# Conditioning weights of one decoder layer loaded and summed for pairs of chunks

## The chip, the cores and the metric

The kernel runs on one core of a Trainium2 chip. The metric is the device time of one execution in microseconds. The median of three runs of the kernel before is 515.8 us (514.55 to 515.91).

## What is computed

One layer of a decoder over 256 tokens of width 1024, all in fp32. What matters here is its first step:

```
mod = silu(c) @ w_ada + b_ada            # w_ada: 1024 x 6144; six parts of 1024: shift1, scale1, gate1, shift2, scale2, gate2
u   = rmsnorm(x, norm1) * (1 + scale1) + shift1
proj = u @ w_in                          # w_in: 1024 x 6848; retention q|k|v|gate, MLA c_q|c_kv|k_rope, two branch gates
...                                      # retention, latent attention, output projections, residual
u2  = rmsnorm(h, norm2) * (1 + scale2) + shift2
h  += gate2 * hier_moe(u2)               # 4 groups of 8 experts, top 1 group, top 2 experts
out = rmsnorm(h, final_norm)
```

The change concerns only shift1 and scale1, the first two parts of mod (columns 0 to 2047 of w_ada).

## The kernel before

SBUF tiles come from 27 slots of 128 partitions by 2048 fp32 (1 MB each), PSUM tiles from 8 banks of 512 columns. All large loads go through one list, `LD`, and are issued by SyncE in the order in which they were added, as soon as a slot is free by a plan made in a first pass over the program. A slot is reused when its last reader is through, so an operation that writes a tile may have to wait for another engine.

The width of 1024 is worked off in eight chunks of 128. For chunk k the early part needs three loads: `("ada", k)`, 128 columns of shift1 and 128 of scale1 of all 1024 rows of w_ada (rows of 512 B, `ld_ada_early`); `("e0", k)`, 704 columns of w_in for c_q, c_kv and k_rope; and `("e1", k)`, 512 columns of w_in for retention's q. They are added in the order ada 0, x, ada 1, e0 0, e1 0, ada 2, e0 1, e1 1, and so on.

`ada_mm(k)` multiplies silu(c) with the loaded columns: eight matmuls of 256 columns, each on one of four groups of 32 columns of the array, so that four partial sums land at partitions 0, 32, 64, 96; DVE copies the bank to `ev`. `mod_of(k)` transposes `ev` (two transposes), and DVE adds the partial sums and makes the chunk's scale `acl` and shift `shc` (a reduction and two small operations). `x_turned(k)` transposes the normed x of the chunk. `u_of(k)` makes u of the chunk on ACT, rounds it to fp32r (`hi`), and DVE subtracts to get the rest (`lo`).

Every product is done as three fp32r matmuls (hi x hi, lo x hi, hi x lo). So each piece of w_in is split first: `split` rounds on ACT and subtracts on DVE (L469, L470). The loop over k (from L541) then does for each chunk: the splits of e0's two halves (352 columns each) and of e1 (512 columns); if there is a next chunk, `x_turned(k + 1)` and `ada_mm(k + 1)`; the products with the first half, `mod_of(k + 1)` and `u_of(k + 1)`, the products with the second half, 12 matmuls of 352 columns in all (L384 to L386); and twelve matmuls of 256 columns with e1 (L536 to L538).

In this stretch TensorE's order is the order of the code. ACT's and DVE's order is chosen by the framework's scheduler, and each of these engines works through its own queue in order. Behind the loop come the units of the middle part (the remaining products of u, attention, retention), then the routing, and the experts, whose weights stream in to the end.

Of the kernel before, what the change touches and what calls it, by code (L numbers as in the profile page):

```python
# [13 lines left out]
AF = mybir.ActivationFunctionType  # L14
ALU = mybir.AluOpType
AX = mybir.AxisListType
# [192 lines left out]
def body(ctx, tc, A, out, plan=None):  # L209
    nc = tc.nc  # L210
    T, V, S, G, Q = nc.tensor, nc.vector, nc.scalar, nc.gpsimd, nc.sync
# [5 lines left out]
    LD = Loads(SL, plan)  # L217
    ring = Ring(SL)

    def bank(name="bank"):  # L220
        return PB.alloc(name)

    w_ada = A["w_ada"][0].rearrange("(k p) n -> p k n", p=128)
# [4 lines left out]
    ev_s = SL.alloc("ev")  # L228
    csb = ev_s.t[:, 1024:1280].rearrange("p (k m) -> p k m", k=8)
# [4 lines left out]
    def row_load(r0, name, n0=0, n=None):  # L234
        v = A[name].rearrange("o n -> (o n)") if len(A[name].shape) == 2 else A[name]
        n = n or v.shape[0]
        S.dma_start(rows[r0:r0 + n // 128, :], v[n0:n0 + n].rearrange("(r c) -> r c", c=128))
# [3 lines left out]
    def ld_ada_early(k):  # L241
        def fn(t):
            v = t.rearrange("p (k s n) -> p k s n", k=8, s=2)
            for s in range(2):
                Q.dma_start(v[:, :, s, :], w_ada[:, :, s * 1024 + k * 128:s * 1024 + (k + 1) * 128])  # L245
        return fn
# [19 lines left out]
    row_load(16, "b_ada", 0, 2048)  # L266
    row_load(32, "q_norm")
    row_load(35, "kv_norm")
    for k in range(8):
        if k < 7:  # L270
            LD.add(("ada", k + 1), ld_ada_early(k + 1))
        LD.add(("e0", k), ld_k(w_in[:, k:k + 1, 4096:4800]))
        LD.add(("e1", k), ld_k(w_in[:, k:k + 1, 0:512]))
    uq = A["w_uq"][0].rearrange("(k p) n -> p k n", p=128)
# [8 lines left out]
    i = 0  # L283
# [78 lines left out]
    def small(n):  # L362
        if sml_n[0] + n > 256:
            sml_n[0] = 0
        a = sml[:, sml_n[0]:sml_n[0] + n]
        sml_n[0] += n
        return a
# [57 lines left out]
    def ada_mm(k, pa):  # L425

        ev = ev_s.t[:, 256 * (k % 2):256 * (k % 2 + 1)]
        t = LD.get(("ada", k)).t.rearrange("p (k n) -> p k n", k=8)
        for j in range(8):
            i = T.matmul(pa.t[32 * (j % 4):32 * (j % 4) + 32, :256], csb[:, j, :], t[:, j, :], start=j < 4, stop=j >= 4,  # L430
                         skip_group_check=True, tile_position=(0, 32 * (j % 4)))
        LD.done(("ada", k))
        V.tensor_copy(ev, pa.t[:, :256])
        return ev, i.ins

    def x_turned(k):
        px = bank()
        for b in range(2):
            T.transpose(px.t[:, b * 128:(b + 1) * 128], xh[:, b, k * 128:(k + 1) * 128], ident)
        return px  # L440

    last_u = [None]
# [1 line left out]
    def mod_of(k, pa, ev):  # L444
        for i in range(2):
            T.transpose(pa.t[:, 256 + i * 128:256 + (i + 1) * 128], ev[:, i * 128:(i + 1) * 128], ident)
        sc = small(2)
        V.tensor_reduce(sc, pa.t[:, 256:512].rearrange("p (i j r) -> p i j r", i=2, j=4)[:, :, :, 0], AX.X, ALU.add)
        V.scalar_tensor_tensor(acl[:, k:k + 1], sc[:, 1:2], bsc1[:, k:k + 1], colt[:, 8 + k:9 + k], op0=ALU.add,
                               op1=ALU.mult)  # L450
        V.tensor_add(shc[:, k:k + 1], sc[:, 0:1], colt[:, 16 + k:17 + k])
        pa.free()

    def u_of(k, px):
        last_u[0] = S.activation(uf[:, k, :], px.t[:, 0:256], AF.Identity, bias=shc[:, k:k + 1], scale=acl[:, k:k + 1]).ins
        hi, lo = hi_lo("u", k)
        S.activation(hi, uf[:, k, :], AF.Copy)
        V.tensor_tensor(lo, uf[:, k, :], hi, ALU.subtract)
        px.free()

    u_blk = blk_of("u")

# [62 lines left out]
    pa = bank()  # L525
# [16 lines left out]
    for k in range(8):  # L542
        hl = hl0 if k == 0 else []
        for w in early_w(k)[len(hl):]:
            hl.append(split(w, 352))
        LD.done(("e0", k))
        hl.append(split(LD.get(("e1", k)).t[:, :512].rearrange("p (k n) -> p k n", k=1), 512))
        LD.done(("e1", k))

        if 0 < k < 7:  # L550
            px, pa = x_turned(k + 1), bank()
            ev = ada_mm(k + 1, pa)[0]
        for n in range(2):
            s, hi, lo = hl[n]
            for b in range(2):
                mm3(eacc[n][b].t[:, :352], u_blk(k, b), (hi[:, 0, :], lo[:, 0, :]), k == 0, k == 7)
            s.free()
            if (n, k) == (0, 0):
                start.close()
                early = ExitStack()  # L560
                early.enter_context(tc.manual_schedule(engines={T.engine}))
                px = x_turned(1)
            if n == (k == 0) and k < 7:
                mod_of(k + 1, pa, ev)
                u_of(k + 1, px)
        if k == 0:
            eacc.append([bank("acc") for _ in range(2)])
        s, hi, lo = hl[2]
        feat_mm(eacc[2], hi[:, 0, :], lo[:, 0, :], *hi_lo("u", k), k)
        s.free()  # L570
    early.close()
    LD.margin = MARGIN[1]
    u_s.free()
# [1185 lines left out]
```

## Time and profile before

| | before |
|---|---|
| median of three runs | 515.8 us |
| profiled execution | 515.37 us, of which the span is 513.7 us |
| TensorE (PE) busy | 486.0 us, 95% of the span |
| VectorE (DVE) busy | 284.0 us, 55% |
| ScalarE (ACT) busy | 199.9 us, 39% |
| bytes moved by DMA | 174.86 MB, 340 GB/s in the mean |
| granted TensorE clock, mean | 0.989 |

The span runs from the first to the last instruction of the profiled execution; what lies around it is 1.67 us. PEld is TensorE's loading of weights, which overlaps its matmuls. A name such as `s<-in_w_ada` says that a tile of the slots was written from the input w_ada.

### The profile page before, as it was taken

To read this page: it belongs to the slowest core of one execution; us is meant where nothing else is said; L and a number is where in the kernel's file an instruction comes from. 1 tells how busy PE (TensorE), PEld (TensorE's weight loads), DVE (VectorE), ACT (ScalarE), POOL (GpSimd) and SP (SyncE) were. 2 spreads that over 40 slices of the span, in tenths; PEclk is the share of its full clock that TensorE was granted. 3 is DMA by queue.
4 is the path that set the end of the run, shared out by engine and by line. 5 is a ranking of instruction groups with operands and counts; after the bars stand their busy time and mean duration, and the time that the engine had idled before them with its cause. 6 is when DMAs were issued, how large, how long until landed. Compare 5 with 4: busy or idle time off the path is not lost.

```text
span 513.7 us, 8596 instructions
## 1 busy us (share of the span) xinstructions
PE 486.0 (95%) x3432; PEld 340.0 (66%) x3432; DVE 284.0 (55%) x529; ACT 199.9 (39%) x371; POOL 61.7 (12%) x59
## 2 busy tenths in 40 slices
PE   6999999999999999999999999999999799979874
PEld 2778999997787888888888887453544445334332
DVE  2555689894696997984777746434333131312013
ACT  2545773553678454456534423122112020112013
POOL 1000322411000002105872000000000000000000
PEclk8999999999999999999999999999999899999998
DMA  9999999888967592899698888999999999999993
GB/s 270 325 318 358 321 327 399 320 291 311 358 226 289 187 385 85 303 385 374 234 365 329 315 356 319 404 417 420 416 420 421 414 417 417 422 419 418 394 342 126
DMA packets 68098, 174.86 MB, mean 340 GB/s; under 512 B 5422, under 2 KB 27091, under 8 KB 57816
## 3 DMA queue, kind: packets, MB, share of 16 engines
q1 hardware_dynamic: 65602, 174.01, 90.6%
q10 hardware_dynamic: 2454, 0.27, 0.4%
q8 instruction: 28, 0.46, 0.4%
q14 instruction: 14, 0.11, 0.1%
HBM read 173.22 MB, written 1.05 MB: 339 GB/s over the span
## 4 chain that ended last, share of the span: by engine, by line
PE 60%; DMA 23%; SPq 6%; DVE 5%; ACT 1%; issue 1%; POOL 1%; ACTq 1%; DVEq 0%; POOLq 0%
DMA s<-in_w 21%; PE b L384 10%; PE b L386 10%; PE b L385 10%; PE b L1442 4%; SPq L253 4%; PE b L1554 3%; PE b L1382 2%; SPq L245 2%; PE b L1565 2%; DMA s<-in_w_in 1%; PE b L538 1%; PE b L537 1%; PE b L536 1%; DVE s L470 1%
## 5 line engine op out<-in xcount | busy, mean ns | idle before, releaser
L470 DVE TENSOR_TENSOR s<-s,s 128x1024 fp32r<-128x1024 f32 (+2 forms) x92 | 103.4, 1136 | 42.9 <-ACT s L469 42.7
L469 ACT ACTIVATE s<-s 128x1024 fp32r<-128x1024 f32 (+2 forms) x92 | 83.5, 923 | 80.1 <-PE b L386 51.0
L384 PE MATMUL b<-s,s 128*128 128x512 f32 (+2 forms) x258 | 101.8, 395 | 1.1 <-ACT s L469 1.0
L386 PE MATMUL b<-s,s 128*128 128x512 f32 (+2 forms) x258 | 98.7, 383 | 0.0
L385 PE MATMUL b<-s,s 128*128 128x512 f32 (+2 forms) x258 | 98.1, 380 | 0.0
L1442 PE MATMUL b<-s,s 128*32 128x256 f32 x1024 | 62.9, 388 | 9.3 <-DMA s<-in_w 7.0
L384 PEld LDWEIGHTS b<-s,s 128*128 128x128 f32 x258 | 48.5, 188 | 15.5 <-ACT s L469 4.4
L1442 PEld LDWEIGHTS b<-s,s 128*32 128x32 f32 x1024 | 34.4, 112 | 36.5 <-DMA s<-in_w 10.6
L386 PEld LDWEIGHTS b<-s,s 128*128 128x128 f32 x258 | 48.4, 188 | 9.7 <-DVE s L470 0.4
L385 PEld LDWEIGHTS b<-s,s 128*128 128x128 f32 x258 | 48.6, 188 | 8.3
L1083 DVE SCALAR_TENSOR_TENSOR s<-s,cs,s 128x1024 f32<-128x1024 f32 x32 | 41.4, 1293 | 0.3
L538 PE MATMUL b<-s,s 128*128 128x256 f32 x128 | 36.2, 284 | 0.4 <-DVE s L470 0.4
L536 PE MATMUL b<-s,s 128*128 128x256 f32 x128 | 36.4, 285 | 0.0
L537 PE MATMUL b<-s,s 128*128 128x256 f32 x128 | 36.1, 283 | 0.0
L1554 PE MATMUL b<-s,wr 128*32 128x512 f32 x224 | 33.9, 596 | 0.6 <-DMA s<-in_w 0.6
L1382 PE MATMUL b<-s,sml 128*128 128x512 f32 x56 | 26.7, 605 | 0.0
L1565 PE MATMUL b<-s,rt 128*128 128x512 f32 x56 | 26.2, 608 | 0.0
L378 ACT ACTIVATE s<-b 128x512 f32<-128x512 f32 (+2 forms) x25 | 14.1, 567 | 29.4 <-PE b L1382 19.6
L380 DVE COPY s<-b 128x512 f32<-128x512 f32 (+2 forms) x13 | 8.1, 625 | 30.6 <-PE b L1382 26.9
L538 PEld LDWEIGHTS b<-s,s 128*128 128x128 f32 x128 | 24.4, 191 | 0.6 <-DVE s L470 0.6
L537 PEld LDWEIGHTS b<-s,s 128*128 128x128 f32 x128 | 24.5, 191 | 0.0
L1707 POOL TENSOR_TENSOR sml<-sml,mhalf 128x1 f32<-128x1 f32 x2 | 1.0, 540 | 195.2 <-DVE sml L1706 195.2
(266 smaller groups left out, 656.7 us busy)
## 6 DMA issues: line engine op xcount, KB each, us to landing
s<-in_w SPq DMA_DIRECT2D x92, 1024.0 KB
s<-in_w_in SPq DMA_DIRECT2D x22, 1024.0 KB
s<-in_w_ada SPq DMA_DIRECT2D x16, 1024.0 KB
s<-in_w_ada SPq DMA_DIRECT2D x16, 512.0 KB
s<-in_w_mla_o SPq DMA_DIRECT2D x4, 1024.0 KB
s<-in_w_ret_o SPq DMA_DIRECT2D x4, 1024.0 KB
s<-in_w_out SPq DMA_DIRECT2D x4, 1024.0 KB
s<-in_w SPq DMA_DIRECT2D x6, 512.0 KB
```

The lines of the kernel that those rows point to most:

```text
L384: T.matmul(o, l[0], r[0], start=start, stop=False, skip_group_check=True)
L385: T.matmul(o, l[1], r[0], start=False, stop=False, skip_group_check=True)
L386: return T.matmul(o, l[0], r[1], start=False, stop=stop, skip_group_check=True)
L469: S.activation(hi, src, AF.Copy)
L470: V.tensor_tensor(lo, src, hi, ALU.subtract)
L536: T.matmul(o, hi[:, f], mh, start=k == 0 and c == 0, stop=False, skip_group_check=True)
L537: T.matmul(o, hi[:, f], ml, start=False, stop=False, skip_group_check=True)
L538: T.matmul(o, lo[:, f], mh, start=False, stop=k == 7, skip_group_check=True)
L1083: V.scalar_tensor_tensor(a, t[:, kk, :], cs[:, k:k + 1], a, op0=ALU.mult, op1=ALU.add)
L1382: T.matmul(pg[k4].t, Sr[:, b], hp[:, b, 4 * k4:4 * k4 + 4, :].rearrange("p k q -> p (k q)"), start=b == 0, stop=b == 1, skip_group_check=True)
L1442: i = T.matmul(ph.t[32 * j:32 * j + 32, 0:256], ug[:, k, 32 * j:32 * j + 32], w, start=k == 0, stop=k == 7, skip_group_check=True, tile_po ...
L1554: T.matmul(py[n].t[32 * j:32 * j + 32, :], hdT[:, k, 32 * j:32 * j + 32], ts[j][:, k, n * 512:(n + 1) * 512], start=k == 0, stop=k == 1, s ...
```

## The change

The chunks 0 and 1 stay as they were. For the pairs (2, 3), (4, 5) and (6, 7), w_ada is loaded as two tiles, each with half of the 1024 rows and 256 columns of either part (rows of 1 KB, `ld_ada_pair`), ahead of the e0 of the pair's first chunk. `ada_pair_mm` sums a pair with eight matmuls of 512 columns, `mod_pair` makes the scales and shifts of both chunks at once, and `x_turned(k, 2)` turns x of both chunks. The sum for chunks 2 and 3 stands in chunk 1, between its products with e0 and those with e1, and `mod_pair(2)` behind chunk 1. The sums for (4, 5) and (6, 7) stand at the start of chunks 3 and 5, and `mod_pair` between the two halves of e0 there. u of the pair's second chunk is asked for in the pair's first chunk.

```diff
--- before.py
+++ after.py
@@ -266,9 +266,19 @@
     row_load(16, "b_ada", 0, 2048)
     row_load(32, "q_norm")
     row_load(35, "kv_norm")
+    def ld_ada_pair(k, h):
+
+        def fn(t):
+            v = t.rearrange("p (k s n) -> p k s n", k=4, s=2)
+            for s in range(2):
+                Q.dma_start(v[:, :, s, :], w_ada[:, 4 * h:4 * h + 4, s * 1024 + k * 128:s * 1024 + (k + 2) * 128])
+        return fn
+
+    LD.add(("ada", 1), ld_ada_early(1))
     for k in range(8):
-        if k < 7:
-            LD.add(("ada", k + 1), ld_ada_early(k + 1))
+        if k in (2, 4, 6):
+            for h in range(2):
+                LD.add(("adap", k, h), ld_ada_pair(k, h))
         LD.add(("e0", k), ld_k(w_in[:, k:k + 1, 4096:4800]))
         LD.add(("e1", k), ld_k(w_in[:, k:k + 1, 0:512]))
     uq = A["w_uq"][0].rearrange("(k p) n -> p k n", p=128)
@@ -433,10 +443,23 @@
         V.tensor_copy(ev, pa.t[:, :256])
         return ev, i.ins
 
-    def x_turned(k):
+    def ada_pair_mm(k, pa):
+
+        ev = ev_s.t[:, 512:1024]
+        for j in range(8):
+            t = LD.get(("adap", k, j // 4)).t.rearrange("p (k n) -> p k n", k=4)
+            T.matmul(pa.t[32 * (j % 4):32 * (j % 4) + 32, :], csb[:, j, :], t[:, j % 4, :], start=j < 4, stop=j >= 4,
+                     skip_group_check=True, tile_position=(0, 32 * (j % 4)))
+        for h in range(2):
+            LD.done(("adap", k, h))
+        V.tensor_copy(ev, pa.t)
+        return ev
+
+    def x_turned(k, n=1):
         px = bank()
-        for b in range(2):
-            T.transpose(px.t[:, b * 128:(b + 1) * 128], xh[:, b, k * 128:(k + 1) * 128], ident)
+        for i in range(n):
+            for b in range(2):
+                T.transpose(px.t[:, i * 256 + b * 128:i * 256 + (b + 1) * 128], xh[:, b, (k + i) * 128:(k + i + 1) * 128], ident)
         return px
 
     last_u = [None]
@@ -451,12 +474,23 @@
         V.tensor_add(shc[:, k:k + 1], sc[:, 0:1], colt[:, 16 + k:17 + k])
         pa.free()
 
-    def u_of(k, px):
-        last_u[0] = S.activation(uf[:, k, :], px.t[:, 0:256], AF.Identity, bias=shc[:, k:k + 1], scale=acl[:, k:k + 1]).ins
+    def mod_pair(k, pa, ev):
+        for i in range(4):
+            T.transpose(pa.t[:, i * 128:(i + 1) * 128], ev[:, i * 128:(i + 1) * 128], ident)
+        sc = small(4)
+        V.tensor_reduce(sc, pa.t.rearrange("p (i j r) -> p i j r", i=4, j=4)[:, :, :, 0], AX.X, ALU.add)
+        V.tensor_add(sc[:, 2:4], sc[:, 2:4], bsc1[:, k:k + 2])
+        V.tensor_mul(acl[:, k:k + 2], sc[:, 2:4], colt[:, 8 + k:10 + k])
+        V.tensor_add(shc[:, k:k + 2], sc[:, 0:2], colt[:, 16 + k:18 + k])
+        pa.free()
+
+    def u_of(k, px, i=0, last=True):
+        last_u[0] = S.activation(uf[:, k, :], px.t[:, i * 256:(i + 1) * 256], AF.Identity, bias=shc[:, k:k + 1], scale=acl[:, k:k + 1]).ins
         hi, lo = hi_lo("u", k)
         S.activation(hi, uf[:, k, :], AF.Copy)
         V.tensor_tensor(lo, uf[:, k, :], hi, ALU.subtract)
-        px.free()
+        if last:
+            px.free()
 
     u_blk = blk_of("u")
 
@@ -547,9 +581,12 @@
         hl.append(split(LD.get(("e1", k)).t[:, :512].rearrange("p (k n) -> p k n", k=1), 512))
         LD.done(("e1", k))
 
-        if 0 < k < 7:
-            px, pa = x_turned(k + 1), bank()
-            ev = ada_mm(k + 1, pa)[0]
+        if k in (2, 4, 6):
+
+            u_of(k + 1, px, 1)
+        if k in (3, 5):
+            px, pa = x_turned(k + 1, 2), bank()
+            ev = ada_pair_mm(k + 1, pa)
         for n in range(2):
             s, hi, lo = hl[n]
             for b in range(2):
@@ -560,14 +597,23 @@
                 early = ExitStack()
                 early.enter_context(tc.manual_schedule(engines={T.engine}))
                 px = x_turned(1)
-            if n == (k == 0) and k < 7:
-                mod_of(k + 1, pa, ev)
-                u_of(k + 1, px)
+            if (k, n) == (0, 1):
+                mod_of(1, pa, ev)
+                u_of(1, px)
+            if (k, n) == (1, 1):
+                px, pa = x_turned(2, 2), bank()
+                ev = ada_pair_mm(2, pa)
+            if k in (3, 5) and n == 0:
+                mod_pair(k + 1, pa, ev)
+                u_of(k + 1, px, 0, False)
         if k == 0:
             eacc.append([bank("acc") for _ in range(2)])
         s, hi, lo = hl[2]
         feat_mm(eacc[2], hi[:, 0, :], lo[:, 0, :], *hi_lo("u", k), k)
         s.free()
+        if k == 1:
+            mod_pair(2, pa, ev)
+            u_of(2, px, 0, False)
     early.close()
     LD.margin = MARGIN[1]
     u_s.free()
```

The order of ACT's queue from the splits of chunk 1 on. In these rows, `s_114` and `s_116` are e0 and e1 of chunk 1, `s_121` and `s_123` those of chunk 2; `s_103` is u and `s_152` its rounded copy. Before:

```order
L469 ACTIVATE s_278<-s_114 128x352
L469 ACTIVATE s_281<-s_114 128x352
L469 ACTIVATE s_284<-s_116 128x512
L455 ACTIVATE s_103<-b_287,shc,acl 128x256
L457 ACTIVATE s_152<-s_103 128x256
L469 ACTIVATE s_336<-s_121 128x352
L469 ACTIVATE s_339<-s_121 128x352
L469 ACTIVATE s_342<-s_123 128x512
L455 ACTIVATE s_103<-b_347,shc,acl 128x256
```

And now, where `s_113` is e1 of chunk 1, `s_121` and `s_123` e0 and e1 of chunk 2, and `s_125` e0 of chunk 3:

```order
L503 ACTIVATE s_284<-s_113 128x512
L503 ACTIVATE s_278<-s_111 128x352
L488 ACTIVATE s_103<-b_247,shc,acl 128x256
L490 ACTIVATE s_152<-s_103 128x256
L503 ACTIVATE s_343<-s_121 128x352
L503 ACTIVATE s_346<-s_121 128x352
L503 ACTIVATE s_349<-s_123 128x512
L503 ACTIVATE s_383<-s_125 128x352
L503 ACTIVATE s_386<-s_125 128x352
L488 ACTIVATE s_103<-b_303,shc,acl 128x256 x2
L490 ACTIVATE s_152<-s_103 128x256 x2
```

Before, u of chunk 2 stands between the splits of chunk 1 and those of chunk 2. Now u of chunk 1 stands behind the splits of its own chunk, and u of chunks 2 and 3 behind the splits of chunk 2 and of chunk 3's e0; both are made before the first is rounded.

TensorE's order around chunk 3 and the start of chunk 4. `b_231` to `b_234` and `b_264`, `b_265` are the accumulators for e0 and e1. Before, where `b_407` is x of chunk 4 and `b_410` takes its sums, and `b_467` is x of chunk 5:

```order
L439 MATMUL b_407<-cst,s_151 128x128 x2
L430 MATMUL b_410<-s_125,s_65 32x256 x8
L384 MATMUL b_231<-s_396,s_152 128x352
...
L386 MATMUL b_232<-s_396,s_152 128x352
L446 MATMUL b_410<-cst,s_65 128x128 x2
L384 MATMUL b_233<-s_399,s_152 128x352
...
L537 MATMUL b_265<-s_152,s_402 128x256
L538 MATMUL b_265<-s_152,s_402 128x256
L439 MATMUL b_467<-cst,s_151 128x128 x2
L430 MATMUL b_470<-s_132,s_65 32x256 x8
L384 MATMUL b_231<-s_456,s_153 128x352
```

And now, where `b_394` is x of chunks 4 and 5, and `b_399` takes their sums:

```order
L462 MATMUL b_394<-cst,s_151 128x128 x4
L451 MATMUL b_399<-s_129,s_65 32x512 x4
L451 MATMUL b_399<-s_132,s_65 32x512 x4
L394 MATMUL b_231<-s_383,s_152 128x352
...
L396 MATMUL b_232<-s_383,s_152 128x352
L479 MATMUL b_399<-cst,s_65 128x128 x4
L394 MATMUL b_233<-s_386,s_152 128x352
...
L572 MATMUL b_265<-s_152,s_389 128x256
L394 MATMUL b_231<-s_450,s_153 128x352
L395 MATMUL b_231<-s_450,s_153 128x352
```

In chunk 3 the places are the same, with twice the columns. Before, two transposes and eight sums stand between the last matmul of chunk 3 (L538) and the first of chunk 4 (L384); now nothing does.

DVE's order from the copy of the sums for chunk 4 to u. Before, where `s_396` to `s_402` are the splits of chunk 3:

```order
L433 COPY s_65<-b_410 128x256
L470 TENSOR_TENSOR s_402<-s_130,s_402 128x512
L448 TENSOR_REDUCE sml<-b_410 128x2
L449 SCALAR_TENSOR_TENSOR acl<-sml,bsc_170,colt 128x1
L451 TENSOR_TENSOR shc<-sml,colt 128x1
L458 TENSOR_TENSOR s_153<-s_103,s_153 128x256
```

And now, where `s_450`, `s_453`, `s_456` are the splits of chunk 4 and `s_490`, `s_493` those of chunk 5's e0:

```order
L455 COPY s_65<-b_399 128x512
L504 TENSOR_TENSOR s_450<-s_135,s_450 128x352
L504 TENSOR_TENSOR s_453<-s_135,s_453 128x352
L481 TENSOR_REDUCE sml<-b_399 128x4
L504 TENSOR_TENSOR s_456<-s_137,s_456 128x512
L482 TENSOR_TENSOR sml<-sml,bsc_170 128x2
L484 TENSOR_TENSOR shc<-sml,colt 128x2
L504 TENSOR_TENSOR s_490<-s_139,s_490 128x352
L483 TENSOR_TENSOR acl<-sml,colt 128x2
L504 TENSOR_TENSOR s_493<-s_139,s_493 128x352
L491 TENSOR_TENSOR s_153<-s_103,s_153 128x256 x2
```

Before, one subtraction of a split stands between the copy of the sums (L433) and the subtraction for u (L458). Now five stand between L455 and L491, four of them ahead of `acl`, the last small operation (L483).

## Rows read from the trace of the kernel before

**Rows 1.** The page, busy tenths in 40 slices of the span.

```profile
PE   6999999999999999999999999999999799979874
...
DMA  9999999888967592899698888999999999999993
```

**Rows 2.** Stretches: length, busy us of PE PEld DVE ACT POOL, clock, DMA, GB/s.

```profile
24.00:29.00 5.00, 3.98 (x35) 2.74 (x34) 2.29 (x7) 1.75 (x4) 0.00 (x0) 1.00 1.15 319
...
34.00:39.00 5.00, 5.00 (x45) 3.92 (x44) 2.71 (x8) 2.26 (x5) 0.00 (x0) 1.00 1.15 318
...
54.60:80.00 25.40, 24.41 (x203) 23.97 (x202) 21.34 (x31) 18.40 (x34) 8.45 (x9) 1.00 0.92 323
...
364.00:493.00 129.00, 118.10 (x1017) 52.51 (x1013) 28.72 (x71) 18.78 (x42) 0.00 (x0) 0.99 1.02 414
```

**Rows 3.** PE's timeline: start us, us, operation, idle time before it.

```profile
26.28 0.43 PE L384 MATMUL b<-s,s 128*128 128x352 f32 x1 [1.02 <-ACT s L469]
...
35.47 0.38 PE L439 MATMUL b<-cst,s 128*128 128x128 f32 x2
35.78 1.07 PE L430 MATMUL b<-s,s 128*32 128x256 f32 x16
36.78 0.43 PE L384 MATMUL b<-s,s 128*128 128x352 f32 x1
...
47.06 0.43 PE L384 MATMUL b<-s,s 128*128 128x352 f32 x1
...
50.94 0.32 PE L384 MATMUL b<-s,s 128*128 128x352 f32 x1
...
53.03 0.28 PE L536 MATMUL b<-s,s 128*128 128x256 f32 x1
...
54.46 0.28 PE L536 MATMUL b<-s,s 128*128 128x256 f32 x1
...
55.51 0.39 PE L538 MATMUL b<-s,s 128*128 128x256 f32 x1 [0.40 <-DVE s L470]
```

**Rows 4.** The chain of waits, early: start us, us, what.

```profile
38.88 7.47 DMA s<-in_w_in
```

**Rows 5.** Stretches of TensorE: busy us, clock, DMA share, GB/s.

```profile
31.20:32.20 1.00, 1.00 (x15) 1.00 1.21 291
...
490.00:494.00 4.00, 3.12 (x37) 1.00 1.08 355
```

**Rows 6.** PE's timeline in the experts, one group of w2.

```profile
328.39 3.64 PE L1554 MATMUL b<-s,wr 128*32 128x512 f32 x32
```

**Rows 7.** Groups by form, DVE, 14 to 54 us: busy us, mean ns.

```profile
L470 DVE TENSOR_TENSOR s<-s,s 128x352 fp32r<-128x352 f32 x16 | 7.8, 522 | 7.8 <-ACT s L469 7.8
L470 DVE TENSOR_TENSOR s<-s,s 128x512 fp32r<-128x512 f32 x8 | 5.5, 685 | 0.7 <-ACT s L469 0.7
...
L451 DVE TENSOR_TENSOR shc<-sml,colt 128x1 f32<-128x1 f32 x7 | 1.1, 153 | 0.0
```

**Rows 8.** The same behind 54 us, copies of 512 columns.

```profile
L380 DVE COPY s<-b 128x512 f32<-128x512 f32 x9 | 6.2, 692 | 28.7 <-PE b L1382 26.9 <-PE b L1301 1.1 <-PE b L1509 0.7
```

**Rows 9.** ACT's timeline: start us, us, operation.

```profile
19.30 1.41 ACT L469 ACTIVATE s<-s 128x352 fp32r<-128x352 f32 x3 [0.16 <-DMA s<-in_w_in]
...
39.09 0.57 ACT L455 ACTIVATE s<-b,shc,acl 128x256 f32<-128x256 f32 x1 [1.53 <-DVE shc L451]
39.69 0.42 ACT L457 ACTIVATE s<-s 128x256 fp32r<-128x256 f32 x1
```

**Rows 10.** Groups by form, ACT, 14 to 54 us.

```profile
L469 ACT ACTIVATE s<-s 128x352 fp32r<-128x352 f32 x16 | 7.2, 489 | 7.8 <-DMA s<-in_w_in 7.7
L469 ACT ACTIVATE s<-s 128x512 fp32r<-128x512 f32 x8 | 5.0, 626 | 0.3 <-PE b L430 0.2
```

**Rows 11.** Stretches of TensorE around a fall of its granted clock.

```profile
403.20:406.60 3.40, 1.12 (x24) 1.00 1.00 410
406.60:410.06 3.46, 3.46 (x40) 0.51 1.01 414
```

## The prediction

> **What bounds the kernel now.** First I read the page's slices [rows 1]: PE stands at 9 tenths from the second slice almost to the end, and DMA is as full while the first loads run. Then the stretches [rows 2]. From 54.6 to 80 us PE works 24.41 of 25.40 us, and it stays so up to the experts. From 364 us DMA fills its share (1.02, 414 GB/s) and PE has pauses. Those transfers start as PE gives tiles back, so what the first 54 us lose or save should reach the end nearly one to one.
>
> So the stretch to price is the early one: eight chunks of u, TensorE starting on the first product behind them at 54.46 us [rows 3]. Its chain of waits is mostly the load queue, and from 38.88 us 7.47 us of w_in transfer [rows 4]; PE however hardly pauses either (5.00 of 5.00 us from 34 to 39, 3.98 from 24 to 29 [rows 2]). One chunk there is 0.31 us of turning x (35.47 to 35.78), 1.00 us of w_ada sums (35.78 to 36.78), then the products; from chunk 4's first product to chunk 6's, 36.78 to 47.06, it is 10.28 us for two chunks [rows 3]. The last chunk, which has no sum, takes 3.52 us (50.94 to 54.46), 2.09 of it before its 256-column products begin at 53.03. PE and DMA are so nearly balanced that a gain in transfers alone cannot be worth much, and a new pause of PE costs its full length.
>
> **What the transfers gain.** Six chunks of w_ada get 1 KB rows in place of 512 B. A stretch of 512 B rows moves 291 GB/s; near the end, where w2's last pieces have 1 KB rows, it is 355 [rows 5]. A chunk's 1.049 MB then takes 2.95 us in place of 3.60: 0.65 us each, 3.9 us for six. The lower bound is no gain, if the 24 KB pitch of w_ada sets the rate. The Trainium skill (DMA: Bandwidth & Descriptors, section Why small descriptors are slow) gives each packet about three cycles on top of one per 32 bytes, hence 19 against 35 cycles for twice the bytes, some 9% more rate. The rows show 22%, so the measurement decides. By that rule I estimate the six chunks to save about 1.7 us.
>
> **What PE's work gains.** A pair's sum is eight matmuls of 512 columns on 32 rows each. The nearest row has sixteen such in 3.64 us [rows 6], so 1.8 us; the upper bound is two sums of before, 2.0. I take 1.8. Transposes keep their columns; four take 0.6 us. So some 0.2 us per pair is saved, 0.6 in all.
>
> **What the new order adds.** Before, PE makes the transposes for chunk k+1's scales between the two halves of chunk k, and behind chunk k's last product it still has the next x and the next sum to do: 1.31 us under which DVE and ACT finish u. Now the transposes of a pair come, on PE, at the end of chunk 1 and in the middle of chunks 3 and 5, and nothing stands between chunk 3 and chunk 4 (or 5 and 6) to cover for u. At the same time the chain to u has become longer, as the three orders show:
> - DVE has, between the copy of the sums and the last scale, three subtractions of 352 and one of 512 columns besides the reduction and three small operations. Copy 0.69 [rows 8], three of 352 at 0.52, one of 512 at 0.69, and four small ones at about 0.15 each (the add that makes shc) [rows 7] make 3.5 us by their durations; neighbours in a queue overlap by some hundredths each, so 3.4.
> - ACT then makes u of both chunks before it rounds the first: in before, the rounding starts 0.60 us behind u (39.09, 39.69) and takes 0.42 [rows 9]; with a second u of about 0.5 us between them it is 1.5 us. A subtraction, which PE's second product wants, is still behind that.
>
> I put the first product of the next even chunk at 5.0 us behind P, the end of the pair's sum: 3.4 + 1.5 and two steps between engines. PE has beside this, in chunk 3 or 5, 2.09 us of 352 columns, at most 0.6 of transposes, 1.43 of 256 columns: 4.1 us. In chunk 1 it has only 1.43 + 0.6 = 2.0 us, since there the sum stands behind the 352-column products. So pauses of about 3 us once and about 1 us twice. Also a split waits for tiles: those of chunk 4 go into the tiles that the pair has just left, which puts chunk 4's e0 behind P; that is inside the 3.4.
>
> **The sum, along PE.** Chunk 1: before, PE was through with the third sum at 25.26 (26.28 less the 1.02 us wait [rows 3]), so chunk 1's first product was some 5.2 us earlier, near 20.1. Now 1.3 us of it is gone from the front, but ACT has three splits (0.49, 0.63, 0.49 [rows 10]) ahead of u of chunk 1, so I start it at 19.5. Its 352 columns end at 21.7 (2.09 and some of the wait for the subtraction); x and sum add 0.6 + 1.8: P is 24.1 and chunk 2 starts at 29.1, against 26.28: **+2.8**. From chunk 2 to chunk 4: 3.6 for chunk 2, 0.6 + 1.8 to P, 5.0 to the product: 11.0, against 10.5 (26.28 to 36.78): **+0.5**. From 4 to 6: 11.0 against 10.28: **+0.7**. Chunks 6 and 7: 3.6 + 3.5 = 7.1, against 7.40 (47.06 to 54.46): **-0.3**. Together +3.7, so the next product starts near 58.2. There PE waited in before for a subtraction, 0.40 us up to 55.51 [rows 3]; as the loads are early now, that pause goes: **-0.4**. That is +3.3; if DVE's and ACT's queues overlap more tightly, by 0.2 us at each of the three boundaries, it is +2.7. I take the middle, **+3.0 us**.
>
> **Are loads late anywhere?** Chunk 1's e0 landed at 19.30 [rows 9]; now 1.049 MB less stand ahead of it, so 15.7. The pair for 2 and 3 then needs 2.36 MB more (e1 too): 22.3 at 355 GB/s, 23.8 at 291. PE comes to its second half at 23.2: at most 0.6 us of wait. Chunk 3's e0, whose split ACT has ahead of u of chunk 2, lands 0.98 MB later, at 25.1 to 27.2, while DVE's chain lets u start at 27.5. The pair for 4 and 5 lands at 31.7 to 35.3, and PE wants its second half at about 34.2. So if rows of 1 KB are no faster, add up to 1 us; if they are, the saved 3.9 us lie beside PE's chain and are worth nothing.
>
> From the profiled execution's 515.37 us (span 513.7 and 1.67 around it) this gives 518.4. The median of the runs shown is 0.43 higher, so **518.8 us**.
>
> **Rivals.**
> - *The clock falls in the new pause.* PE at 1.12 us busy of 3.40 is followed by 3.46 us at a granted clock of 0.51, that is 1.2 GHz in place of 2.4, while 3.98 of 5.00 is not [rows 2, 11]. A pause of 3 us behind chunk 1 comes near the first. 3.46 us at half speed lose 1.7 us: 520.5. The Trainium skill (TensorE: Matmul & The Clock Gate, section Part 1: The HAM clock gate) also has the array go back to its half clock when it idles. Against it: the pause is bounded on both sides by dense work.
> - *Transfers bound the stretch and PE's pauses hide behind them.* The chain of waits [rows 4] speaks for it. Then the 3.9 us are gained: 511.9, and the kernel is faster. It decides if ACT and DVE reach u before PE is through with chunks 1, 3 and 5, that is if the 5.0 us behind P are under 2.0 in chunk 1. Against it: PE works 5 us of 5 in most of the stretch, and the chain of DVE and ACT is made of measured pieces.
> - *Both cancel.* If chain and pauses come out at half (0.5 us per boundary less, chunk 2 at +1.2), the end is about +0.7: 516.5. For it: engines' queues overlap neighbours more than single durations say.
> - *The later part takes the delay up*, because loads run ahead while PE pauses. Against it: PE is the one that is full until past 300 us [rows 1], so early data are no use to it. This too would be 516 or less.
>
> **How the numbers follow.** Changes under 0.3% (1.55 us) can't be told from none here. The forecast has 0.62, the clock's fall 0.14, cancelling or taking up 0.15, transfers 0.09. Forecast and clock are slower than 517.35 but for a thin part: slower 0.75, within 0.3% 0.16, faster 0.09. The likeliest case alone runs from 517.4 to 520.0. For 8 in 10 the range goes down to 515.3, through most of the cancelling case, and up to 521.3, past the clock's fall with a late pair.
>
> **What would show it.** Right: a PE pause of 2 to 3.5 us ahead of chunk 2's first product (about 29 us), with ACT's rounding of u as releaser; pauses near 1 us ahead of chunks 4 and 6; the first product behind the chunks at 57 to 58.5 us; w_ada stretches at about 350 GB/s; and stretches behind it that are as long as before. Wrong: a first product behind the chunks at 54.5 us or earlier, pauses that end on DMA, or a shift at 55 us that isn't there at 300.

## The result, and the profile after

The changed kernel takes **523.53 us** (median of five runs, 522.50 to 523.96), against 515.8 us for the kernel before in the same session (514.55 to 516.14): a ratio of 1.0158, 95% interval 1.0147 to 1.0168. It is slower, as forecast, but by about 8 us and not by 3, and the time lies outside the range. The profiled execution took 523.13 us, of which 521.4 are the span, 7.7 more than before.

The page's slices of the changed kernel, which answer to [rows 1]:

```profile
PE   7988979999999999999999999999999997989884
...
DMA  9999896769957696599698989899999999999994
```

DMA, which before stood at 8 and 9 over the first eleven slices, now falls to 6 and 7 in the seventh to ninth (78 to 117 us), which would fit loads that are ahead of PE and wait for tiles; this was not followed further. PE shows 8s in the third and fourth slice and a 7 in the sixth (65 to 78 us), where before it had 9s.

The stretches of the changed kernel, in the columns of [rows 2]: the early one, the one at 74 us in the middle part (before, PE worked 4.00 of 4.00 us there), two in which the clock was at half, and one of w_ada's 1 KB rows, which answers to [rows 5]:

```profile
24.00:29.00 5.00, 2.58 (x24) 1.96 (x17) 3.49 (x11) 3.23 (x8) 0.00 (x0) 0.99 1.08 354
...
74.00:78.00 4.00, 2.07 (x10) 1.87 (x11) 4.00 (x8) 3.38 (x7) 0.00 (x0) 0.84 1.04 405
...
28.93:32.35 3.42, 3.41 (x11) 3.24 (x12) 1.16 (x3) 0.89 (x2) 0.00 (x0) 0.50 1.08 370
76.72:80.13 3.41, 3.41 (x18) 3.41 (x18) 3.41 (x6) 0.77 (x2) 0.09 (x1) 0.50 1.03 380
...
36.00:38.00 2.00, 2.00 (x19) 1.56 (x12) 1.44 (x3) 1.00 (x3) 0.00 (x0) 1.00 1.09 349
```

From 24 to 29 us PE works 2.58 us where it worked 3.98. For 3.42 us from 28.93 and again for 3.41 from 76.72 the granted clock is 0.50, that is 1.2 GHz in place of 2.4, with PE busy all through; by estimate such a stretch can cost half its length, 1.7 us. w_ada moves 349 GB/s, as the prediction had it.

PE's timeline of the changed kernel, answering to [rows 3, 6]. The first four rows are the first products of chunks 2, 4 and 6 and the first 256-column product of chunk 7, the fifth is the first product behind the chunks; L835 to L889 lie in the MLA preparation behind the chunks; the last is the group of w2 of [rows 6]:

```profile
28.94 0.66 PE L394 MATMUL b<-s,s 128*128 128x352 f32 x1 [2.42 <-ACT s L490]
...
41.41 0.43 PE L394 MATMUL b<-s,s 128*128 128x352 f32 x1 [0.91 <-ACT s L490]
...
52.12 0.43 PE L394 MATMUL b<-s,s 128*128 128x352 f32 x1 [0.50 <-ACT s L490]
...
57.81 0.28 PE L570 MATMUL b<-s,s 128*128 128x256 f32 x1
...
59.25 0.28 PE L570 MATMUL b<-s,s 128*128 128x256 f32 x1
...
69.19 1.20 PE L835 MATMUL b<-cst,s 128*128 128x128 f32 x9 [0.74 <-ACT s L818]
...
74.39 0.39 PE L888 MATMUL b<-s,s 128*128 128x256 f32 x1 [0.81 <-DVE s L844]
...
76.43 0.39 PE L889 MATMUL b<-s,s 128*128 128x256 f32 x1 [1.54 <-DVE s L860]
...
336.54 3.64 PE L1600 MATMUL b<-s,wr 128*32 128x512 f32 x32
```

| first product of | before | predicted | after |
|---|---|---|---|
| chunk 2 | 26.28 | 29.1 | 28.94 |
| chunk 4 (distance) | 36.78 (10.50) | (11.0) | 41.41 (12.47) |
| chunk 6 (distance) | 47.06 (10.28) | (11.0) | 52.12 (10.71) |
| chunk 7, 256 columns (distance) | 53.03 (5.97) | (5.7) | 57.81 (5.69) |
| behind the chunks | 54.46 | 57 to 58.5 | 59.25 |
| group of w2 | 328.39 | | 336.54 |

So the delay is 2.66 us at chunk 2, 4.78 at the end of the chunks and 8.15 in the experts, and it is 8.2 already at 94 us. There are two losses. The second, 3.4 us, arises between 66 and 81 us: pauses of 0.74, 0.81 and 1.54 us (3.09), less 1.4 us that the kernel before lost behind its chunks (0.40 at 55.51 [rows 3], and by its waits 0.6 and 0.4 in the MLA preparation), make 1.7; the other 1.7 is what the half clock costs by the estimate above.

What makes PE wait there is seen on POOL, DVE and ACT. The timelines of the changed kernel, POOL, then DVE, then ACT. L723 is the first of POOL's two operations for a rope (a rotation by position). The MLA norms take two steps from the sums of squares: a multiply and add on DVE (L383) and a power on POOL (L384). L818 is ACT's scaling by them, L504 the subtraction of a split:

```profile
60.56 1.50 POOL L723 TENSOR_TENSOR s<-s 128x256 f32<-128x256 f32 x1 [5.88 <-ACT s L807]
...
64.16 0.85 POOL L723 TENSOR_TENSOR s<-s 128x256 f32<-128x256 f32 x1 [1.40 <-DVE sml L383]
...
65.72 2.36 POOL L384 TENSOR_TENSOR sml<-sml,mhalf 128x2 f32<-128x2 f32 x2
...
63.99 0.23 DVE L383 TENSOR_SCALAR sml<-sml 128x2 f32<-128x2 f32 x2
...
65.08 1.76 DVE L504 TENSOR_TENSOR s<-s,s 128x1024 fp32r<-128x1024 f32 x1
...
67.45 0.62 ACT L818 ACTIVATE s<-s,sml 128x384 f32<-128x384 f32 x1 [4.06 <-POOL sml L384]
```

And the same places of the kernel before, where the multiply and add is L373, the powers are L374, the rope L677, the scaling L772:

```profile
56.78 0.70 POOL L374 TENSOR_TENSOR sml<-sml,mhalf 128x2 f32<-128x2 f32 x1 [7.38 <-DVE sml L373]
58.86 0.69 POOL L374 TENSOR_TENSOR sml<-sml,mhalf 128x2 f32<-128x2 f32 x1 [1.37 <-DVE sml L373]
60.20 1.50 POOL L677 TENSOR_TENSOR s<-s 128x256 f32<-128x256 f32 x1 [0.65 <-DVE s L676]
...
58.62 0.16 DVE L373 TENSOR_SCALAR sml<-sml 128x2 f32<-128x2 f32 x1
...
58.14 0.61 ACT L772 ACTIVATE s<-s,sml 128x384 f32<-128x384 f32 x1
```

Before, both powers stand ahead of the rope's operations, and ACT scales from 58.14 us. Now ACT has the sums of squares ready at 60.75 us, but DVE comes to its multiply and add only at 63.99, behind its own operations for two ropes, and POOL to the first power at 65.72, behind both ropes; ACT idles 4.06 us for it and scales from 67.45. Of these 6.7 us some 3.2 are DVE's queue and some 1.6 POOL's; the first power, beside DVE's subtraction at 65.08, takes 1.7 us where it took 0.70 before. The code there is unchanged; what moved is the order that the scheduler chose for DVE and POOL.

### The profile page after: what moved, and what is told of

It reads as the page before. It is cut to its first block, busy times and chain, and to the rows that moved or that the text cites. A ratio compares the mean times of both kernels' runs of the same rounds, so it can differ in the third digit from the quotient of the medians.

```text
span 521.4 us, 8487 instructions
## 1 busy us (share of the span) xinstructions
PE 490.8 (94%) x3381; PEld 342.5 (66%) x3384; DVE 283.1 (54%) x520; ACT 199.2 (38%) x371; POOL 63.9 (12%) x59
## 5 line engine op out<-in xcount | busy, mean ns | idle before, releaser
L504 DVE TENSOR_TENSOR s<-s,s 128x1024 fp32r<-128x1024 f32 (+2 forms) x92 | 104.2, 1143 | 40.9 <-ACT s L503 40.7
L1488 PE MATMUL b<-s,s 128*32 128x256 f32 x1024 | 65.9, 402 | 7.8 <-DMA s<-in_w 7.8
L394 PEld LDWEIGHTS b<-s,s 128*128 128x128 f32 x258 | 49.0, 190 | 18.9 <-ACT s L490 5.2
L395 PEld LDWEIGHTS b<-s,s 128*128 128x128 f32 x258 | 49.1, 190 | 9.1 <-DVE s L491 1.0
L396 PEld LDWEIGHTS b<-s,s 128*128 128x128 f32 x258 | 49.0, 190 | 8.9
L570 PEld LDWEIGHTS b<-s,s 128*128 128x128 f32 x128 | 24.5, 191 | 0.9 <-issue 0.8
L571 PEld LDWEIGHTS b<-s,s 128*128 128x128 f32 x128 | 24.5, 192 | 0.0
L572 PEld LDWEIGHTS b<-s,s 128*128 128x128 f32 x128 | 24.5, 192 | 0.0
```

The source lines that it names most:

```text
L394: T.matmul(o, l[0], r[0], start=start, stop=False, skip_group_check=True)
L395: T.matmul(o, l[1], r[0], start=False, stop=False, skip_group_check=True)
L396: return T.matmul(o, l[0], r[1], start=False, stop=stop, skip_group_check=True)
L504: V.tensor_tensor(lo, src, hi, ALU.subtract)
L570: T.matmul(o, hi[:, f], mh, start=k == 0 and c == 0, stop=False, skip_group_check=True)
L571: T.matmul(o, hi[:, f], ml, start=False, stop=False, skip_group_check=True)
```

## The experiments

Theory A: two losses, an early one made of the serial chain from a pair's sum to the next product and of the clock that falls in its pause, and a second one made by the order of DVE and POOL in the MLA preparation. The rivals: the early delay or late loads cause the later waits; the clock costs nothing, since DVE and ACT set the boundaries anyhow; the transfers set the early stretch. All times are medians, with the ratio to the kernel before on the same chip and its 95% interval; kernels of different sessions are better compared by their ratios.

**norms_first.** One step of the MLA preparation is issued ahead of the first rope.

```diff
-SIDE = [0, 0, 3, 1, ...
+SIDE = [0, 0, 2, 1, ...
...
+    step(mla_it)
     rope_q0 = rope_post("q", 0)
```

> The changed kernel with one step of the MLA preparation (the sums of squares, whose reciprocal roots DVE and POOL compute) issued before the first rope instead of behind it. Theory A (the second loss, from +4.8 us at 64 us to +8.5 near 80 us, comes from DVE and POOL standing at rope operations while ACT waits 4.06 us for POOL's power): that wait goes, PE's pauses at 66 to 81 us shrink from about 3 us to 1 or less, the half clock at 76.7 us with them, and the time is 3 to 4.5 us under the changed kernel: 519 to 520.5 us. Rival (the early delay lets something else run late there, loads or tiles, and the order only shows it): PE's pauses stay, 523 to 524 us.

Measured: 519.95 us, ratio 1.0086 (1.0071 to 1.0100), 3.6 us under the changed kernel. Its timelines, POOL and then PE:

```profile
59.91 0.70 POOL L384 TENSOR_TENSOR sml<-sml,mhalf 128x2 f32<-128x2 f32 x1 [5.63 <-DVE sml L383]
...
61.44 1.68 POOL L384 TENSOR_TENSOR sml<-sml,mhalf 128x2 f32<-128x2 f32 x1
...
72.73 0.39 PE L889 MATMUL b<-s,s 128*128 128x256 f32 x1 [0.66 <-DVE s L860]
...
87.29 0.66 PE L920 MATMUL b<-cst,s 128*128 128x128 f32 x4 [0.98 <-DVE s L910]
```

The powers run at 59.91 and 61.44 us, and PE's three pauses have become two, 1.64 us in all. At 100 us PE is 4.39 us behind the kernel before, as it is at the end of the chunks: the second loss is gone and the first is left. The early delay is nearly the same here (chunk 2 at 28.72 us), so the rival is out.

**before_norms_late.** The opposite, on the kernel before: only the order in the MLA preparation is spoilt. `last_rope` holds the last rope operation of DVE and of POOL, and the norms' steps are issued behind both.

```diff
-        rsqrt(r4[:, 0:2], ...)
-        rsqrt(r4[:, 2:4], ...)
+        with tc.issue_after(last_rope[0]), tc.issue_after(last_rope[1]):
+            rsqrt(r4[:, 0:2], ...)
+            rsqrt(r4[:, 2:4], ...)
```

> The kernel before, with only this order given to it: the first operations of the MLA preparation's reciprocal roots on DVE and on POOL are issued behind the last rope operation of that engine. The chunks are untouched. Theory A: ACT waits for POOL near 60 to 64 us, PE pauses some 3 us there and may fall to half clock, and the time is 518.5 to 520.5 us. Rival (the order costs nothing when the chunks are on time): 515.5 to 516.5 us.

Measured: 518.45 us, ratio 1.0063 (1.0051 to 1.0075). Its timelines, POOL and PE, and then its stretches:

```profile
65.72 1.56 POOL L374 TENSOR_TENSOR sml<-sml,mhalf 128x2 f32<-128x2 f32 x2
...
67.31 0.44 PE L793 MATMUL b<-cst,s 128*128 128x128 f32 x2 [2.71 <-ACT s L776]
```

```profile
66.00:70.00 4.00, 2.69 (x17) 2.51 (x18) 0.55 (x2) 3.30 (x7) 1.28 (x2) 0.83 1.04 406
70.00:74.00 4.00, 4.00 (x28) 4.00 (x27) 3.76 (x8) 3.83 (x8) 0.00 (x0) 0.75 1.01 353
```

The order alone, with the chunks on time, costs some 3 us: a pause of 2.71 us and a stretch at half clock behind it, the pattern of the changed kernel. DVE's and POOL's order were changed together, so what each costs alone is not shown.

**warm_gap** and **norms_warm.** Eight dummy products fill the pause ahead of chunk 2; the second of the two has the norms' step first as well.

```diff
             mod_pair(2, pa, ev)
+            keep_warm(8)
             u_of(2, px, 0, False)
```

> The changed kernel with eight dummy products put on PE behind the sum of chunks 2 and 3, in the pause before chunk 2's first product. Clock theory (the 2.42 us pause there brings the half clock from 28.93 to 32.35 us, worth 1.7 us): chunk 2's products run at full clock, chunk 4 starts 1.5 us or so earlier, the time is about 521.8 us. Rival (only the pause counts, the chain of DVE and ACT sets the later boundaries as well): the clock is full and the products behind the chunks begin no earlier than 59 us; 523 to 524 us.

> The changed kernel with the norms' step first and the eight dummy products in the pause before chunk 2. With the norms' step alone the clock still falls to half at 28.7 us and the early delay is +4.4 us. Clock theory: chunk 2 to chunk 4 takes 11.1 us instead of 12.3, and the time is 1.2 to 1.7 us under that kernel: 518.2 to 518.8 us. Rival (the later boundaries, set by DVE and ACT, take the saved time up): 519.5 to 520.3 us.

Measured: warm_gap 523.38 us (1.0155, 1.0142 to 1.0168), norms_warm 518.91 us (1.0077, 1.0064 to 1.0090). PE's and ACT's timelines of warm_gap, and a stretch of norms_warm:

```profile
29.84 0.43 PE L394 MATMUL b<-s,s 128*128 128x352 f32 x1 [0.22 <-ACT s L490]
...
40.96 0.42 PE L394 MATMUL b<-s,s 128*128 128x352 f32 x1 [0.92 <-ACT s L490]
...
11.17 0.63 ACT L538 ACTIVATE s<-s 128x512 f32<-128x512 f32 x1 [1.95 <-DMA s<-in_x]
```

```profile
28.88:32.28 3.40, 3.37 (x21) 3.13 (x22) 1.44 (x3) 0.89 (x2) 0.00 (x0) 1.00 1.08 368
```

In both, the clock stays at 1.00 behind the dummies, and from chunk 2 to chunk 4 it is 11.12 and 11.13 us, in place of 12.47 in the changed kernel and 12.28 in norms_first: the fall costs 1.2 to 1.3 us there. No later boundary in the chunks takes it up: from chunk 4 to the last chunk's 256 columns it is 16.4 us in all four. Behind them norms_warm gives back some of it: it is 1.0 us ahead of norms_first at those columns and 0.6 us at the group of w2 (332.14 against 332.73). Its ratio is lower by 0.0009, some 0.5 us, less than the clock theory had, and the two intervals overlap: the time alone doesn't show the gain. warm_gap doesn't show it in its time at all. In its profiled execution the second half of x landed 1.5 us later than in the changed kernel, and the first products began 1.1 us later; whether that was so in its other runs can't be seen, so by its time alone warm_gap is inconclusive.

**rows512.** The longer rows alone are undone.

```diff
-                Q.dma_start(v[:, :, s, :], w_ada[:, 4 * h:4 * h + 4, s * 1024 + k * 128:s * 1024 + (k + 2) * 128])
+                for c in range(2):
+                    Q.dma_start(v[:, :, s, c * 128:(c + 1) * 128], w_ada[:, 4 * h:4 * h + 4, s * 1024 + (k + c) * 128:s * 1024 + (k + c + 1) * 128])
```

> The changed kernel with the pair tiles loaded in rows of 512 B (two transfers of 128 columns for each part), all else as it is: only the longer rows are undone. Theory (the transfers' gain lies beside PE's chain): the w_ada stretches fall from about 350 to about 290 GB/s, chunk 2's first product moves by at most 1 us, and the time is 523 to 524.8 us. Rival (transfers set the early stretch): each pair is 1.3 us later, 3 us or more in all: 526.5 us or above.

Measured: 524.36 us (1.0169, 1.0155 to 1.0182), 0.8 us over the changed kernel. Its stretches, and its timelines of ACT, DVE and PE:

```profile
17.00:19.00 2.00, 1.86 (x16) 1.63 (x14) 1.78 (x7) 1.69 (x4) 0.00 (x0) 1.00 1.21 290
...
29.10:32.50 3.40, 3.36 (x21) 3.12 (x22) 1.44 (x3) 0.89 (x2) 0.00 (x0) 1.00 1.16 283
```

```profile
47.81 1.40 ACT L504 ACTIVATE s<-s 128x352 fp32r<-128x352 f32 x3 [4.64 <-DMA s<-in_w_in]
...
48.34 0.53 DVE L505 TENSOR_TENSOR s<-s,s 128x352 fp32r<-128x352 f32 x1 [4.45 <-ACT s L504]
48.78 0.68 DVE L456 COPY s<-b 128x512 f32<-128x512 f32 x1
...
49.52 0.66 PE L480 MATMUL b<-cst,s 128*128 128x128 f32 x4 [1.18 <-DVE s L456]
```

With 512 B rows the rate is 290 GB/s. The pause ahead of chunk 2 is 2.41 us, as in the changed kernel, yet the clock stays at 1.00 from 29.10. The loads are late instead: PE waits 0.82 us for w_ada at 35.29 us, ACT waits 4.64 us for e0, DVE's copy of the finished sums stands behind that e0's subtraction (48.34, 48.78), and PE waits 1.18 us for it. From chunk 2 to the last chunk's 256 columns it is 29.65 us here and 27.53 in warm_gap, both at full clock. In the changed kernel, with the fall of its clock, it is 28.87. So by the profiled executions the longer rows are worth about 2 us in this order of work, of which the fall took back 1.3. That lies between theory and rival; that the time lies in the theory's range is, by this account, the luck of a clock that stayed up here.

**by_hand, order_only, split_only.** DVE and ACT are kept in code order in the chunk loop (order_only); the splits of the next even chunk's e0 are written right behind the pair's sum (split_only); both (by_hand). `split_e0` makes the splits of a chunk's e0.

```diff
-                early.enter_context(tc.manual_schedule(engines={T.engine}))
+                early.enter_context(tc.manual_schedule(engines={T.engine, V.engine, S.engine}))
...
             ev = ada_pair_mm(k + 1, pa)
+            ahead = split_e0(k + 1, [])
```

> The changed kernel with DVE's and ACT's work in the chunk loop kept in the order of the code, and the splits of the next even chunk's e0 made right behind the pair's sum. Chain theory (the early +4.8 us is the serial chain from the pair's sum over DVE's subtractions and scales and ACT's two u to the next product): the chain gets shorter, chunk 2's first product comes near 28.2 us, the pauses ahead of chunks 4 and 6 go, the products behind the chunks start near 55.5 us instead of 59.25: 519.5 to 520.5 us if the loss in the MLA preparation stays, about 516.5 if it goes with the earlier start. Rival (the loads of the pair set those boundaries): no boundary moves by more than 0.5 us, 523 to 524 us.

> The changed kernel with DVE and ACT in the order of the code in the chunk loop, and nothing else (the splits of e0 are made at the head of their chunk, so behind the scales and u of that chunk). If the order alone gives by_hand its 8.3 us, it is 515 to 516.5 us. If the splits' place matters as much, the boundaries pause for the splits instead (0.49 us of ACT and 0.52 us of DVE more behind u at each of three): 516.5 to 518 us, and more if the clock falls.

> The changed kernel with the next even chunk's e0 splits written right behind the pair's sum, DVE and ACT left to the scheduler. If the place of the splits in the code is what by_hand gained from: 515 to 517 us. If the order on DVE and ACT is (the scheduler had put the splits there already): chunk 2 near 28.9 us, the MLA preparation late as in the changed kernel, 522 to 524 us.

| | time, us | ratio (95%) | chunk 2 | chunk 4 | chunk 6 | chunk 7, 256 columns | group of w2 |
|---|---|---|---|---|---|---|---|
| changed kernel | 523.53 | 1.0158 (1.0147 to 1.0168) | 28.94 | 41.41 | 52.12 | 57.81 | 336.54 |
| order_only | 518.53 | 1.0058 (1.0036 to 1.0080) | 28.28 | 38.28 | 48.48 | 54.11 | 329.86 |
| split_only | 516.65 | 1.0031 (1.0017 to 1.0044) | 28.98 | 40.19 | 50.42 | 56.12 | 329.73 |
| by_hand | 515.26 | 1.0002 (0.9989 to 1.0014) | 28.30 | 38.35 | 48.01 | 53.29 | 326.86 |

My expectation for split_only was wrong: I held that the scheduler had put the splits there already. DVE's timeline of the changed kernel, from the copy of the sums for chunks 4 and 5 to their scale:

```profile
36.56 0.69 DVE L455 COPY s<-b 128x512 f32<-128x512 f32 x1 [3.93 <-PE b L451]
37.17 0.95 DVE L504 TENSOR_TENSOR s<-s,s 128x352 fp32r<-128x352 f32 x2
38.14 0.17 DVE L481 TENSOR_REDUCE sml<-b 128x4 f32<-128x16 f32 x1
38.66 0.69 DVE L504 TENSOR_TENSOR s<-s,s 128x512 fp32r<-128x512 f32 x1 [0.35 <-ACT s L503]
39.27 0.15 DVE L482 TENSOR_TENSOR sml<-sml,bsc 128x2 f32<-128x2 f32 x1
39.34 0.15 DVE L484 TENSOR_TENSOR shc<-sml,colt 128x2 f32<-128x2 f32 x1
39.41 0.52 DVE L504 TENSOR_TENSOR s<-s,s 128x352 fp32r<-128x352 f32 x1
39.85 0.15 DVE L483 TENSOR_TENSOR acl<-sml,colt 128x2 f32<-128x2 f32 x1
```

And the same end of split_only's, from the reduction on, with POOL's powers behind it:

```profile
37.98 0.17 DVE L481 TENSOR_REDUCE sml<-b 128x4 f32<-128x16 f32 x1
38.19 0.16 DVE L482 TENSOR_TENSOR sml<-sml,bsc 128x2 f32<-128x2 f32 x1
...
38.38 0.16 DVE L483 TENSOR_TENSOR acl<-sml,colt 128x2 f32<-128x2 f32 x1
...
59.04 0.71 POOL L384 TENSOR_TENSOR sml<-sml,mhalf 128x2 f32<-128x2 f32 x1 [6.06 <-DVE sml L383]
...
62.06 0.70 POOL L384 TENSOR_TENSOR sml<-sml,mhalf 128x2 f32<-128x2 f32 x1
```

In the changed kernel a subtraction of 512 and one of 352 columns stand between the reduction and the scale, which is ready 3.4 us behind the copy's start; in split_only they don't, and it is 2.1 us. The pause ahead of chunk 4 goes, the one ahead of chunk 6 shrinks to 0.19 us, and in the MLA preparation the powers stand at 59.04 and 62.06 us, with no wait of PE left from 58 us on. Nothing was edited there: the place of a split 10 us and more ahead decides how the scheduler orders DVE and POOL behind the loop. order_only comes to its last chunk's 256 columns 2.0 us ahead of split_only and loses that in the preparation, where PE still waits 1.1 and 0.4 us (its second power runs at 64.55 us): at the group of w2 the two are level. Its median is 1.9 us higher even so, above both cases that I had written down; its runs spread from 516.41 to 519.54 us and the two intervals overlap, so that they differ is not shown. by_hand has both edits: the whole loss is gone, and the time is that of the kernel before (I had expected 516.5). At the group of w2 its profiled execution, 513.85 us, is 1.5 us ahead of the kernel before; its median doesn't keep that lead. Beside 0.59 us ahead of chunk 1, one pause is left in its chunks, ahead of chunk 2:

```profile
28.30 0.43 PE L394 MATMUL b<-s,s 128*128 128x352 f32 x1 [1.83 <-ACT s L490]
```

**by_hand_norms, before_norms_first, before_order.** Controls: by_hand with norms_first's step; that step on the kernel before; code order for DVE and ACT on the kernel before.

> Both edits, the chunk loop's order by hand and the norms' step ahead of the first rope. If the two losses are separate, their gains add: 3.6 us measured for the norms' step and 3 to 4 us for the chunks: 516 to 517 us. If they are one loss seen twice, no more than the better of the two alone: 519.5 to 520 us.

> Control: the kernel before with the norms' step ahead of the first rope. If the step gains 3.6 us in the changed kernel only because it puts an order right that the change had upset, it does nothing here: 515 to 516.3 us. If it is a gain of its own, whatever the chunks do: 512 to 513.5 us.

> Control: the kernel before with DVE and ACT in the order of the code in the chunk loop. If by_hand only takes back what the change lost, the order is worth nothing here: 515 to 516.5 us. If code order is a gain of its own in this loop, 512.5 to 514 us, and by_hand still has a loss from the pairs in it.

Measured: 515.16 us (1.0001, 0.9991 to 1.0011), 514.70 us (0.9990, 0.9981 to 0.9999) and 516.66 us (1.0030, 1.0020 to 1.0040). Where the order is right already, the norms' step gains 0.1% or less, so its 3.6 us were repair, or nearly so. The gains of by_hand and norms_first don't add: by_hand's order had mended the second loss too. Code order is no gain of its own; on the kernel before it costs 1.4 us.

**pairs_from4.** by_hand, with chunks 2 and 3 loaded and summed one by one as before.

```diff
-        if k in (2, 4, 6):
+        if k in (1, 2):
+            LD.add(("ada", k + 1), ld_ada_early(k + 1))
+        if k in (4, 6):
...
```

> By_hand with pairs only for chunks 4 and 5, 6 and 7; chunks 2 and 3 are loaded and summed one at a time as before. By_hand's only pause at a boundary is the 1.83 us ahead of chunk 2. Theory (a pair whose sum stands late in the chunk ahead can't be covered, the two later ones can): chunk 2 at 26.3 us in place of 28.3, the products behind the chunks 1.3 to 2 us earlier, 513.3 to 514.2 us, faster than both kernels. Rival (what is gained there is lost to the loads, whose 512 B rows cost 0.65 us more in each of two chunks): 515 to 515.5 us.

Measured: 514.50 us (0.9985, 0.9975 to 0.9995), the lowest of these medians and under both kernels, though within 0.3% of the kernel before, and its interval overlaps by_hand's. Chunk 2 starts at 26.98 us, without a pause (its first chunk started 1.4 us later than by_hand's, 16.23 against 14.87); now the load is late for the sum of chunks 4 and 5:

```profile
34.08 1.06 PE L453 MATMUL b<-s,s 128*32 128x512 f32 x8 [1.61 <-DMA s<-in_w_ada]
```

So theory and rival each have a part: the boundary is mended, and 1.61 us of what it gave go to a wait for w_ada.

## Why the prediction was wrong

**Right.** Three of the four early terms, worked out from rows of the kernel before, hold: chunk 2 at +2.66 us (predicted +2.8), chunk 4 to 6 +0.43 (+0.7), chunks 6 and 7 -0.28 (-0.3). The pauses end on ACT's rounding of u, as the text said, and the wait at 55.51 us is gone (-0.4). Some of the closeness is luck. At chunk 2 two errors cancel in part: the pair's sum ended at 24.38 us (24.1), and the next product came 4.56 us behind it (5.0); ahead of chunks 4 and 6 it came 4.98 and 4.56 us behind it. DVE's chain was 3.4 us, as summed, only ahead of chunk 4, and 0.35 us of it was a wait for ACT that the sum hadn't; ahead of chunks 2 and 6 it was 3.0 and 2.9 us. With the clock kept up, in norms_warm, the chunks end 3.39 us late against the +3.7 of the sum before its two deductions.

**Wrong, the step that decided it:** "stretches behind it that are as long as before". The stretch from 66 to 81 us became 3.4 us longer. The sum has no term for the order of the engines behind the chunks, so it put it at nothing without a reason. I had followed the new order on DVE and ACT inside the chunks and not behind them, where the scheduler had put DVE's and POOL's steps for the norms behind both ropes. norms_first takes 3.6 us back, and its 519.95 us would have lain in the range; before_norms_late makes such a loss by order alone. That "what the first 54 us lose or save should reach the end nearly one to one" held, taken by itself: norms_first is 4.39 us late at the end of its chunks and 4.5 us slower. It was not the whole loss.

**Wrong in its chance:** the clock's fall was a rival at 0.14, with the argument that dense work lies on both sides of the pause. It fell all the same, in the changed kernel, norms_first and split_only. This is where the fourth early term failed: chunk 2 to chunk 4 took 12.47 us, +1.97 in place of +0.5, and the first product behind the chunks came at 59.25 us and not at 57 to 58.5. The fall's price, 1.7 us, was 1.2 to 1.5 there (12.28 less 11.13, 12.47 less 11.12, or less the 11.0 predicted).

**Wrong in size:** what the rows of 512 B would cost. Without the longer rows PE's boundaries pause for loads, about 2 us at like clock; I had allowed up to 1 us for it.

In steps from kernel to kernel, by the ratios, it is 4.0 us for the chain (norms_warm over the kernel before), 0.5 for the clock (norms_first over norms_warm, whose intervals overlap) and 3.7 for the order (the changed kernel over norms_first), the half clock behind its pauses included. Such steps add up to the whole, 8.1 us, by construction. The range was too narrow because every case in it kept the middle part as it was or let it take time up.

## What to carry to other kernels

Where a scheduler orders engines, an edit's price includes the order it brings about elsewhere: read each engine's new queue to its end, the lightly loaded ones too, since two tiny operations on DVE and two on POOL, issued behind the ropes, cost 3 us here (before_norms_late). When sums for two steps are made at once, ask what lies on PE between the sum and the first product that wants it; if less than the chain over DVE and ACT, write what is not of that chain ahead of it. A pause of TensorE of the length seen here is to be priced with a stretch at half clock behind it as an equal case, not as a remote one: of the six pauses of 2.2 to 2.7 us in the first 70 us, four had one.

## What the runs showed of the hardware

The length of a pause alone didn't tell whether the clock falls: behind 2.42 or 2.43 us without products it was at half for some 3.4 us in three kernels (0.50 to 0.56 in the mean), and it fell behind 2.71 us in before_norms_late; behind 2.41 us in rows512 and 2.22 us in order_only it stayed at 1.00. What else decides was not tried. Behind 1.83 us, in by_hand, it stayed up too.

How long a power on POOL takes goes with what DVE does beside it. In five kernels one of the two powers started while a subtraction of 1024 columns ran on DVE: it took 1.67 to 1.70 us, and the subtraction 1.75 to 1.76 in place of 1.22. The other 23 powers of the fourteen profiled executions took 0.69 to 0.89. No run changed this alone, and the spans on POOL are rough.

In two of the fourteen profiled executions (warm_gap, pairs_from4) the first chunk's products began at 16.1 and 16.2 us, in the others between 14.6 and 15.0, though the loads ahead of them are the same. In warm_gap it was x that landed late; in pairs_from4 x was on time, and the cause wasn't followed.
